# Two stages of an encoder layer: quadrant sums in scratch tiles, the first FFN set's weights split earlier

## The chip, the cores and the metric

The kernel runs on one core of one Trainium2 chip. The metric is the device time of one execution in microseconds (us). The kernel before takes 1883.55 us, the median of three runs (1881.67 to 1885.08).

## What is computed

The reference is a two-layer encoder over 512 tokens of width 1024, all in float32. Each layer mixes tokens with three kinds of attention, gates and merges them, and goes on so:

```python
mix = jnp.einsum('bsd,de->bse', merged, w_out[l])
x = layer_norm(DN_ALPHA * x + mix, ln1_g[l], ln1_b[l])
gu = jnp.einsum('bsd,df->bsf', x, w_ffn_in[l])
hidden = jax.nn.silu(gu[..., :D_FF]) * gu[..., D_FF:]
ffn = jnp.einsum('bsf,fd->bsd', hidden, w_ffn_out[l])
x = layer_norm(DN_ALPHA * x + ffn, ln2_g[l], ln2_b[l])
```

D_FF is 2816. The change lies between the first of these lines and the fourth.

## The kernel before, in words

**Number format.** Every matrix operand is split in two float32r parts, hi and lo, and a product is three matmuls: hi·hi, hi·lo and lo·hi (`mm3`, L158 to L161; `product`, L737 to L747). A split is a copy to hi on ScalarE and a subtraction to lo on VectorE. `split` (L189 to L195) does it in program order; `wsplit` (L137 to L143) does it for weights, into tiles `whi` and `wlo` of 1024 columns, four of each, and at high priority.

**Buffers.** Weights are loaded on SyncE's queue into tiles `raw` of 1024 columns, of which there are two (L127), or, in the fast FFN sets, into slots of H. H is a list of 8 slots of 1024 columns and R one of 38 slots of 512 columns (class `Slots`, L61 to L77): `get` takes the slot that was put back first, `put` appends. Scratch tiles P (`ptile`, L122) have 512 columns, four of them. PSUM banks have tags (`acc`, `sc`, `pv`, `tr`), two banks each. The framework adds the semaphores, and orders each engine's instructions by priority, which is program order unless raised, and by its own estimate of when they can start.

**Output projection** (`out_proj`, L670 to L681). It runs over two halves of 512 output columns; for each it loads four pieces of `w_out`, and for each of four token tiles runs 24 matmuls of 512 columns, 192 in all. The result is added to the residual `xt`, four slots of H that were reloaded before. `yield` hands a finished token tile of the second half to the norm.

**Norm** (`layer_norm`, L204 to L223, then `to_xt`, L228 to L234). For each token tile VectorE takes statistics, GpSimd computes the inverse root (L201, L202) and a shift (L214, L215), and the 1024 columns are scaled in two ways: the first 512 on VectorE (L222, L223), the others on ScalarE (L217) and GpSimd (L218, multiply by the gain; L219, add the bias). Gain and bias are two more slots of H (L240). TensorE then transposes the tile in two groups (L233), and ScalarE and VectorE split it (L191, L192) into `xth` and `xtl`, which hold the transposed activations.

**FFN.** The 22 blocks of 128 hidden columns are worked off in eleven sets of two, in chunks of 3, 3, 3 and 2 sets (L926). Set 0 is plain (`ffn_plain`, L758): four weight pieces through `raw` and `wsplit`, then 192 matmuls of 256 columns, for each half of the tokens first gate, then up, then `hidden` (L749). It needs the first two token tiles for its first half only. The other ten sets are fast (`ffn_fast`, L775): seven products of 24 matmuls of 256 columns in place of eight, in the manner of Strassen and Winograd. Three products read a quadrant of x itself (`from_x`), four read one of four sums of quadrants (`from_sum`: t1 to t4); the weights are combined as well: `s = u0 + u1`, `u0 = g0 - u0`, `g0 = s - g0` (L797 to L799, high priority), later `g1 = g1 - g0`. A set loads `g0`, `u0`, `u1` into H, takes `s` from H, and loads `g1` into `raw`.

**The sums** (`x_sums`, L699 to L729) are computed once per layer, after set 0: nine VectorE operations of 1024 columns on three slots of H, and eight splits of 512 columns, in the order t2, t1, t3, t4. The three slots go back to H at L728, after the last split, so the slots that `ffn_fast` takes next (L789, L790) are in part these.

Of the kernel before, what the change touches and what calls it, by code (L numbers as in the profile page):

```python
# [9 lines left out]
F32 = mybir.dt.float32  # L10
# [74 lines left out]
def trunk(ctx, tc, x, ln_in, w_in, feat, bias, lamv, w_mla, w_mlr, w_mlv, w_branch, w_out,  # L85
# [93 lines left out]
    class KTiles:  # L179
# [5 lines left out]
        def __getitem__(self, key):  # L185
            p, k, c = key
            return self.tiles[k][p, c]

# [481 lines left out]
    def out_proj(xt, mg, l):  # L670
        act = tuple(KTiles(m) for m in mg)
        for hf in range(2):
            c = slice(hf * 512, (hf + 1) * 512)
# [25 lines left out]
    def x_sums():  # L699

        four = lambda t: t.rearrange("p (k c) -> p k c", k=4)
        h = lambda kh, th: f32(quad(xth, kh, th))
        lo = lambda kh, th: f32(quad(xtl, kh, th))
        ts = [H.get() for _ in range(3)]
        t1, t2, d = (four(t) for t in ts)

        def halves(t):
            res = []
            for i in range(2):
                hl = (R.get(), R.get())  # L710
                split(*hl, t[:, i * 512:(i + 1) * 512])
                res.append(hl)
            return res

        V.tensor_sub(t1, h(0, 1), h(0, 0))
        V.tensor_sub(d, lo(0, 1), lo(0, 0))
        V.tensor_add(t1, t1, d)
        V.tensor_sub(t2, h(1, 1), t1)
        V.tensor_add(t2, t2, lo(1, 1))
        s2 = halves(ts[1])  # L720
        s1 = halves(ts[0])
        V.tensor_sub(d, t2, h(0, 0))
        V.tensor_sub(d, d, lo(0, 0))
        s3 = halves(ts[2])
        V.tensor_sub(t1, h(1, 0), t2)
        V.tensor_add(t1, t1, lo(1, 0))
        s4 = halves(ts[0])
        H.put(*ts)  # L728
        return s1, s2, s3, s4  # L729
# [28 lines left out]
    def ffn_plain(l, m):  # L758

        chs = []  # L760
        for base in (0, D_FF):
            c = slice(base + m * 128, base + (m + 2) * 128)
            chs.append(wload_ks(lambda a, e: [w_ffn_in[l, a:e, c]], 256, (4, 4)))
# [3 lines left out]
        for h in range(2):  # L767
# [4 lines left out]
            res.append(hidden(pg[h], pu[h]))  # L772
        return res

    def ffn_fast(l, m, sums):  # L775
# [19 lines left out]
        A.activation(p1, px, AF.Copy)  # L795
        with tc.high_priority():
# [11 lines left out]
        product(px, halved(g1), from_x(1, 0), False)  # L808
# [30 lines left out]
    for l in range(DEPTH):  # L839
# [81 lines left out]
        for t in out_proj(xt, mg, l):  # L921
# [4 lines left out]
        for c, (m0, n) in enumerate(CHUNKS):  # L926
            sets = []
            for i in range(n):
                m = 2 * (m0 + i)
                if m0 + i == 0:  # L930
                    sets.append(ffn_plain(l, m))
                    sums = x_sums()
                else:
                    sets.append(ffn_fast(l, m, sums))
# [107 lines left out]
```

## Time and profile before

| what | value |
|---|---|
| median of three runs | 1883.55 us |
| the profiled execution | 1883.03 us |
| its span, first to last instruction | 1881.3 us |
| mean granted TensorE clock | 0.989 of full |
| TensorE busy, matmul | 1817.8 us, 97% |
| VectorE busy | 1323.6 us, 70% |
| ScalarE busy | 911.9 us, 48% |
| GpSimd busy | 135.7 us, 7% |
| DMA, share of 16 engines | 34.2% |

In the profile PE is TensorE's matmul, PEld its weight load, DVE is VectorE, ACT ScalarE, POOL GpSimd and SP SyncE. A line such as L142 is a line of the kernel; the helpers' lines (L141, L142, L191, L192) serve many callers, so the tile names tell the stage. Matmul durations overlap, so starts tell the rate. "Idle before" with an arrow is the time that the engine stood still ahead of an instruction, and what ended it.

### The profile page before, as it was taken

To read this page: it belongs to the slowest core of one execution; us is meant where nothing else is said; L and a number is where in the kernel's file an instruction comes from. 1 tells how busy PE (TensorE), PEld (TensorE's weight loads), DVE (VectorE), ACT (ScalarE), POOL (GpSimd) and SP (SyncE) were. 2 spreads that over 40 slices of the span, in tenths; PEclk is the share of its full clock that TensorE was granted. 3 is DMA by queue.
4 is the path that set the end of the run, shared out by engine and by line. 5 is a ranking of instruction groups with operands and counts; after the bars stand their busy time and mean duration, and the time that the engine had idled before them with its cause. 6 is when DMAs were issued, how large, how long until landed. Compare 5 with 4: busy or idle time off the path is not lost.

```text
span 1881.3 us, 28600 instructions
## 1 busy us (share of the span) xinstructions
PE 1817.8 (97%) x11200; PEld 1621.9 (86%) x11200; DVE 1323.6 (70%) x2172; ACT 911.9 (48%) x1621; POOL 135.7 (7%) x217
## 2 busy tenths in 40 slices
PE   7999999999997899999999999999999979999997
PEld 5988899988887899999879888999888779999995
DVE  6488886666558877777646888766656578676766
ACT  3567776555424433333236677755554244333430
POOL 4100000000003000000031000000000210000001
PEclk9999999999999899999999999999999989999999
DMA  7453333233232232323355332322233223333331
GB/s 251 117 164 95 90 84 84 74 84 94 86 129 79 90 113 90 115 88 106 110 154 159 118 96 86 91 67 81 81 100 130 84 74 121 109 96 108 100 98 71
DMA packets 167767, 195.88 MB, mean 104 GB/s; under 512 B 8528, under 2 KB 132688, under 8 KB 167632
## 3 DMA queue, kind: packets, MB, share of 16 engines
q1 hardware_dynamic: 167632, 194.05, 34.2%
q8 instruction: 88, 1.44, 0.3%
q14 instruction: 47, 0.39, 0.1%
HBM read 177.24 MB, written 9.44 MB: 99 GB/s over the span
## 4 chain that ended last, share of the span: by engine, by line
PE 88%; DVE 5%; DMA 2%; issue 2%; ACT 1%; POOL 1%; SPq 0%; POOLq 0%; DVEq 0%; ACTq 0%
PE acc L159 18%; PE acc L160 18%; PE acc L161 18%; PE sc L746 11%; PE pv L746 8%; PE tr L617 2%; DVE wlo L142 1%; PE pv L460 1%; DMA f<-in_w_ffn_in_dram 1%; PE sc L446 1%; PE pv L625 1%; PE pv L624 1%; PE sc L601 1%; PE sc L600 1%; PE sc L602 1%
## 5 line engine op out<-in xcount | busy, mean ns | idle before, releaser
L141 ACT ACTIVATE whi<-raw 128x1024 fp32r<-128x1024 f32 (+4 forms) x254 | 262.5, 1034 | 292.9 <-PE acc L161 63.8
L142 DVE TENSOR_TENSOR wlo<-raw,whi 128x1024 fp32r<-128x1024 f32 (+4 forms) x254 | 304.8, 1201 | 136.3 <-ACT whi L141 133.2
L159 PE MATMUL acc<-xth,whi 128*128 128x512 f32 x512 | 204.0, 399 | 0.1
L141 ACT ACTIVATE whi<-f 128x1024 fp32r<-128x1024 f32 x100 | 104.5, 1056 | 204.8 <-PE acc L161 102.3
L160 PE MATMUL acc<-xtl,whi 128*128 128x512 f32 x512 | 202.6, 396 | 0.0
L161 PE MATMUL acc<-xth,wlo 128*128 128x512 f32 x512 | 202.6, 396 | 0.0
L746 PE MATMUL pv<-r,whi 128*128 128x256 f32 x960 | 177.3, 284 | 23.7 <-ACT whi L141 22.5
L160 PE MATMUL acc<-wlo,r 128*128 128x512 f32 (+1 forms) x504 | 196.4, 390 | 0.0
L161 PE MATMUL acc<-whi,r 128*128 128x512 f32 (+1 forms) x504 | 196.4, 390 | 0.0
L159 PE MATMUL acc<-whi,r 128*128 128x512 f32 (+1 forms) x504 | 193.8, 390 | 2.3 <-DVE f L831 1.5
L159 PE MATMUL acc<-whi,xth 128*128 128x256 f32 (+2 forms) x576 | 174.9, 305 | 2.4 <-ACT whi L141 1.6
L160 PE MATMUL acc<-wlo,xth 128*128 128x256 f32 (+2 forms) x576 | 175.7, 306 | 1.0 <-DVE wlo L142 0.8
L161 PE MATMUL acc<-whi,xtl 128*128 128x256 f32 (+2 forms) x576 | 176.0, 306 | 0.0
L746 PEld LDWEIGHTS pv<-r,whi 128*128 128x128 f32 x960 | 150.0, 191 | 26.4 <-ACT whi L141 22.9
L142 DVE TENSOR_TENSOR wlo<-f,whi 128x1024 fp32r<-128x1024 f32 x100 | 121.2, 1222 | 31.0 <-ACT whi L141 31.0
L746 PE MATMUL pv<-r,wlo 128*128 128x256 f32 x480 | 135.7, 283 | 0.0
L746 PE MATMUL sc<-xth,whi 128*128 128x256 f32 x480 | 133.9, 280 | 0.0
L746 PE MATMUL sc<-xtl,whi 128*128 128x256 f32 x480 | 133.8, 279 | 0.0
L746 PE MATMUL sc<-xth,wlo 128*128 128x256 f32 x480 | 133.1, 279 | 0.0
L201 POOL TENSOR_SCALAR ring<-ring 128x1 f32<-128x1 f32 x68 | 26.3, 387 | 1417.2 <-ACT otmp L466 811.7
L159 PEld LDWEIGHTS acc<-whi,xth 128*128 128x128 f32 x576 | 109.1, 190 | 7.2 <-ACT whi L141 2.0
L160 PEld LDWEIGHTS acc<-wlo,xth 128*128 128x128 f32 x576 | 109.2, 190 | 6.4 <-DVE wlo L142 2.1
(225 smaller groups left out, 4308.5 us busy)
## 6 DMA issues: line engine op xcount, KB each, us to landing
raw<-in_w_in_dram SPq DMA_DIRECT2D x64, 512.0 KB, 3.8
f<-in_w_ffn_in_dram SPq DMA_DIRECT2D x60, 512.0 KB, 3.6
raw<-in_w_ffn_out_dram SPq DMA_DIRECT2D x44, 512.0 KB, 3.8
raw<-in_w_in_dram SPq DMA_DIRECT2D x64, 256.0 KB, 3.3
raw<-in_w_ffn_in_dram SPq DMA_DIRECT2D x28, 512.0 KB, 3.6
raw<-in_w_branch_dram SPq DMA_DIRECT2D x24, 512.0 KB, 3.5
raw<-in_w_out_dram SPq DMA_DIRECT2D x16, 512.0 KB, 3.9
r<-r SPq DMA_DIRECT2D x56, 128.0 KB, 2.9
```

The lines of the kernel that those rows point to most:

```text
L141: A.activation(hi[:, :n], raw[:, :n], AF.Copy)
L142: V.tensor_sub(lo[:, :n], raw[:, :n], f32(hi[:, :n]))
L159: T.matmul(o, lh[0], rh[0], start=first, stop=False)
L160: T.matmul(o, lh[0], rh[1], start=False, stop=False)
L161: T.matmul(o, lh[1], rh[0], start=False, stop=last)
L201: G.tensor_scalar(dst, src, eps, None, op0=OP.add)
L446: T.matmul(sc, qs[j][:, tsl(t)], ks[j][1], start=False, stop=True)
L460: T.matmul(po[:, 0:256], ch_[:, tsl(k)], v, start=k == 0, stop=False)
L600: T.matmul(sc, q[0][:, tsl(t)], k[0], start=True, stop=False)
L601: T.matmul(sc, q[0][:, tsl(t)], k[1], start=False, stop=False)
L617: T.transpose(pt[:, tsl(i)], prs[i % 2][:, tsl(kp + i // 2)], ident)
L746: T.matmul(o[:, c], w[a][:, j, f], x[e], start=fresh and mi == 0 and j == 0 and n == 0, stop=j == 3 and n == 2, skip_group_check=True)
```

## The change

The sums are computed in two rounds (i = 0, 1), each over two of the four blocks of 128 in a quadrant, in three scratch tiles P of 512 columns instead of three slots of H. The weights of set 0 are loaded and split by a new function at the start of the second half of `out_proj`, into 16 slots of R, two operations of 512 columns per piece, in place of `whi` and `wlo`; the slots go back to R when set 0 is done. In the first fast set only, the first product with `g1` moves from fifth to second place. The diff, without the unchanged lines between:

```diff
+    class Pairs:
+        def __init__(self, tiles, ncol):
+            self.tiles, self.ncol = tiles, ncol
+        def __getitem__(self, key):
+            p, k, c = key
+            a = k % 2 * self.ncol
+            return self.tiles[k // 2][p, a + c.start:a + c.stop]
+    def wload_slots(src_of, ncol, steps):
+        res, slots, k = [], [], 0
+        for n in steps:
+            raw = wp.tile([128, 1024], F32, tag="raw", name="raw", bufs=2)
+            rv = raw[:, :n * ncol].rearrange("p (k c) -> p k c", k=n)
+            c = 0
+            for src in src_of(k * 128, (k + n) * 128):
+                w = src.shape[1]
+                nc.sync.dma_start(rv[:, :, c:c + w], src.rearrange("(k p) c -> p k c", p=128))
+                c += w
+            hl = ([], [])
+            for a in range(0, n * ncol, 512):
+                hi, lo = R.get(), R.get()
+                split(hi, lo, raw[:, a:a + 512])
+                hl[0].append(hi)
+                hl[1].append(lo)
+            slots += hl[0] + hl[1]
+            res.append((k, n, tuple(Pairs(i, ncol) for i in hl)))
+            k += n
+        return res, slots
...
     def gate_tiles():
         return [dp.tile([128, 512], F32, tag="gt", name="gt", bufs=2) for _ in range(2)]
 
-    def out_proj(xt, mg, l):
+    def out_proj(xt, mg, l, ahead):
         act = tuple(KTiles(m) for m in mg)
         for hf in range(2):
+            if hf == 1:
+                ahead()
             c = slice(hf * 512, (hf + 1) * 512)
             ch = wload_ks(lambda a, e: [w_out[l, a:e, c]], 512, (2, 2, 2, 2))
             for t in range(NT):
...
 
     def x_sums():
 
-        four = lambda t: t.rearrange("p (k c) -> p k c", k=4)
         h = lambda kh, th: f32(quad(xth, kh, th))
         lo = lambda kh, th: f32(quad(xtl, kh, th))
-        ts = [H.get() for _ in range(3)]
-        t1, t2, d = (four(t) for t in ts)
-        def halves(t):
-            res = []
-            for i in range(2):
+        two = lambda t: t.rearrange("p (k c) -> p k c", k=2)
+        res = [[], [], [], []]
+        for i in range(2):
+            ts = [ptile() for _ in range(3)]
+            t1, t2, d = (two(t) for t in ts)
+            q = lambda a: a[:, 2 * i:2 * i + 2]
+            def halves(n, t):
                 hl = (R.get(), R.get())
-                split(*hl, t[:, i * 512:(i + 1) * 512])
-                res.append(hl)
-            return res
-        V.tensor_sub(t1, h(0, 1), h(0, 0))
-        V.tensor_sub(d, lo(0, 1), lo(0, 0))
-        V.tensor_add(t1, t1, d)
-        V.tensor_sub(t2, h(1, 1), t1)
-        V.tensor_add(t2, t2, lo(1, 1))
-        s2 = halves(ts[1])
-        s1 = halves(ts[0])
-        V.tensor_sub(d, t2, h(0, 0))
-        V.tensor_sub(d, d, lo(0, 0))
-        s3 = halves(ts[2])
-        V.tensor_sub(t1, h(1, 0), t2)
-        V.tensor_add(t1, t1, lo(1, 0))
-        s4 = halves(ts[0])
-        H.put(*ts)
-        return s1, s2, s3, s4
+                split(*hl, t)
+                res[n].append(hl)
+            V.tensor_sub(t1, q(h(0, 1)), q(h(0, 0)))
+            V.tensor_sub(d, q(lo(0, 1)), q(lo(0, 0)))
+            V.tensor_add(t1, t1, d)
+            V.tensor_sub(t2, q(h(1, 1)), t1)
+            V.tensor_add(t2, t2, q(lo(1, 1)))
+            halves(1, ts[1])
+            halves(0, ts[0])
+            V.tensor_sub(d, t2, q(h(0, 0)))
+            V.tensor_sub(d, d, q(lo(0, 0)))
+            halves(2, ts[2])
+            V.tensor_sub(t1, q(h(1, 0)), t2)
+            V.tensor_add(t1, t1, q(lo(1, 0)))
+            halves(3, ts[0])
+        return res
 
     def from_x(kh, th):
         return lambda j: (quad(xth, kh, th)[:, j], quad(xtl, kh, th)[:, j])
...
         split(*hl, sg)
         return hl
 
-    def ffn_plain(l, m):
-        chs = []
+    def plain_weights(l, m):
+        chs, slots = [], []
         for base in (0, D_FF):
             c = slice(base + m * 128, base + (m + 2) * 128)
-            chs.append(wload_ks(lambda a, e: [w_ffn_in[l, a:e, c]], 256, (4, 4)))
+            ch, sl = wload_slots(lambda a, e: [w_ffn_in[l, a:e, c]], 256, (4, 4))
+            chs.append(ch)
+            slots += sl
+        return chs, slots
+    def ffn_plain(chs, slots):
         pg = [bank("sc"), bank("sc")]
         pu = [bank("pv"), bank("pv")]
         res = []
...
                     gemm_w(pp[h][:, mi * 256:(mi + 1) * 256], w, slice(mi * 128, (mi + 1) * 128), XT,
                            slice(h * 256, (h + 1) * 256), KD)
             res.append(hidden(pg[h], pu[h]))
+        R.put(*slots)
         return res
 
-    def ffn_fast(l, m, sums):
+    def ffn_fast(l, m, sums, early):
 
 
         t1, t2, t3, t4 = sums
...
         product(px, halved(g0), from_x(0, 0), True)
         p1 = ptile()
         A.activation(p1, px, AF.Copy)
+        if early:
+            product(px, halved(g1), from_x(1, 0), False)
         with tc.high_priority():
             V.tensor_add(s, u0, u1)
             V.tensor_sub(u0, g0, u0)
...
         u3 = ptile()
         V.tensor_add(u3, py, p1)
         V.tensor_add(u3, pz, u3)
-        product(px, halved(g1), from_x(1, 0), False)
+        if not early:
+            product(px, halved(g1), from_x(1, 0), False)
         with tc.high_priority():
             V.tensor_sub(g1, g1, g0)
         product(pz, halved(g1), from_x(1, 1), False)
...
             xt.append(H.get())
             nc.sync.dma_start(xt[t], xd[t])
         gb = load_gb(ln1[l])
-        for t in out_proj(xt, mg, l):
+        plain = []
+        for t in out_proj(xt, mg, l, lambda: plain.append(plain_weights(l, 0))):
             layer_norm(xt[t], *gb, spread=SP1[t])
             to_xt(xt[t], t)
         H.put(*gb)
...
             for i in range(n):
                 m = 2 * (m0 + i)
                 if m0 + i == 0:
-                    sets.append(ffn_plain(l, m))
+                    sets.append(ffn_plain(*plain[0]))
                     sums = x_sums()
                 else:
-                    sets.append(ffn_fast(l, m, sums))
+                    sets.append(ffn_fast(l, m, sums, m0 + i == 1))
                 if done is not None and i < 2:
                     for _ in ffn_down(l, *done, xt, c == 1, i):
                         pass
```

## Rows read from the trace of the kernel before

**Rows 1.** The page: chain that ended last by engine; a tensor's DMA issues

```profile
PE 88%; DVE 5%; DMA 2%; issue 2%; ACT 1%; POOL 1%; SPq 0%; POOLq 0%; DVEq 0%; ACTq 0%
...
raw<-in_w_out_dram SPq DMA_DIRECT2D x16, 512.0 KB, 3.9
```

**Rows 2.** Waits of the whole run: engine, line, releaser, us in total, times, longest us

```profile
PE pv L746 <- ACT whi L141: 22.5, 2, 11.3
```

**Rows 3.** Timeline of TensorE: start us, us, what, idle before and its releaser

```profile
576.29 0.39 PE L159 MATMUL sc<-xth,whi 128*128 128x256 f32 x1 [3.25 <-ACT xth L191]
...
616.21 0.58 PE L746 MATMUL pv<-r,whi 128*128 128x256 f32 x1 [11.33 <-ACT whi L141]
...
947.54 0.69 PE L233 MATMUL tr<-cons,f 128*128 128x128 f32 x2 [3.21 <-DVE xtl L192]
```

**Rows 4.** Stretches: us; busy us of PE, PEld, DVE, ACT, POOL; granted clock; DMA share; GB/s

```profile
526.80:572.60 45.80, 45.80 (x203) 36.80 (x202) 25.31 (x34) 10.52 (x12) 10.30 (x14) 1.00 0.24 79
575.00:580.00 5.00, 3.51 (x26) 3.08 (x27) 4.75 (x6) 4.29 (x6) 2.57 (x2) 1.00 0.35 105
588.00:608.00 20.00, 16.89 (x144) 16.68 (x142) 19.46 (x24) 8.30 (x14) 0.00 (x0) 1.00 0.15 50
608.00:616.00 8.00, 0.00 (x0) 0.00 (x0) 3.84 (x4) 0.90 (x1) 0.00 (x0) 0.56 0.21 66
616.00:623.00 7.00, 6.63 (x30) 6.34 (x31) 6.17 (x6) 3.48 (x5) 0.00 (x0) 0.53 0.44 131
623.00:660.00 37.00, 37.00 (x317) 37.00 (x316) 31.42 (x35) 17.68 (x21) 0.00 (x0) 1.00 0.29 90
```

**Rows 5.** Chain that ended last, in order of time: start us, us, what

```profile
598.81 1.14 DVE f L722
...
605.15 2.42 DVE r L192 x4
...
607.59 3.48 DMA f<-in_w_ffn_in_dram
...
611.20 1.24 DVE f L797
...
617.96 4.69 PE pv L746 x22
...
626.36 2.83 PE pv L746 x24
```

**Rows 6.** Timeline of SyncE's queue: start us, us, what

```profile
523.63 0.38 SPq L132 DMA_DIRECT2D raw<-in_w_out_dram  x1
...
553.96 21.25 SPq L132 DMA_DIRECT2D raw<-in_w_ffn_in_dram  x4
...
586.44 36.04 SPq L782 DMA_DIRECT2D f<-in_w_ffn_in_dram  x6
```

**Rows 7.** Timeline of GpSimd in the norm: start us, us, what, idle before

```profile
561.90 0.57 POOL L202 TENSOR_TENSOR ring<-ring,expo 128x1 f32<-128x1 f32 x1
...
570.34 1.55 POOL L202 TENSOR_TENSOR ring<-ring,expo 128x1 f32<-128x1 f32 x1
...
583.65 1.39 POOL L218 TENSOR_TENSOR f<-f,f 128x512 f32<-128x512 f32 x1 [0.94 <-ACT f L217]
```

**Rows 8.** Timeline of VectorE in the norm and at the sums' start

```profile
569.99 1.47 DVE L142 TENSOR_TENSOR wlo<-raw,whi 128x1024 fp32r<-128x1024 f32 x1 [1.10 <-ACT whi L141]
...
587.68 0.69 DVE L192 TENSOR_TENSOR xtl<-tr,xth 128x512 fp32r<-128x512 f32 x1 [3.79 <-ACT xth L191]
588.29 1.22 DVE L715 TENSOR_TENSOR f<-xth 128x1024 f32<-128x1024 f32 x1
```

**Rows 9.** Groups by form, 584 to 625: shapes, count, busy us, mean ns, idle before

```profile
L192 DVE TENSOR_TENSOR r<-f,r 128x512 fp32r<-128x512 f32 x8 | 5.1, 685 | 0.0
...
L191 ACT ACTIVATE r<-f 128x512 fp32r<-128x512 f32 x8 | 4.7, 622 | 4.9 <-DVE f L723 4.4 <-DVE f L717 0.5
```

**Rows 10.** Timeline of ScalarE in the projection: start us, us, what, idle before

```profile
545.20 1.06 ACT L141 ACTIVATE whi<-raw 128x1024 fp32r<-128x1024 f32 x1 [14.84 <-PE acc L161]
```

## The prediction, made before the change was run

> **What bounds the kernel now.** The page comes first: TensorE carries 88% of the chain that ended last [rows 1]. A change off TensorE's path gives nothing, so I looked for the places where TensorE stands still. The waits name the longest: `product` (L746) waits for a weight split on ScalarE twice, 22.5 us together, 11.3 us the longest, once in each layer [rows 2]; in order of time it ends at 616.21 in layer 0 [rows 3]. [...] A smaller stop lies ahead of it: the first FFN matmul, at 576.29, waits 3.25 us for ScalarE to split a transposed block [rows 3].
>
> The chain in order of time says why the long stop exists [rows 5]. The last four splits of `x_sums` end at 607.6; only then can the load of `u0` be issued, since `x_sums` held three slots of H and `u0` and `u1` take two of them. The load costs 3.48 us, three VectorE additions of 1.24 us follow from 611.20, then a ScalarE copy, and TensorE starts again. VectorE was not the cause in the end: of 608 to 616 it works 3.84 us [rows 4]. SyncE shows the same from the other side: six loads spread over the 36 us after 586.44, held for slots [rows 6].
>
> **The change, part by part** (layer 0; the waits say that layer 1 stops as long).
>
> 1. Sums in scratch tiles instead of H. Following the slot queue by hand, four of H's eight slots hold the residual and two the norm's gain and bias at this place; two are free, last used by the merges. Now `g0` and `u0` get those two, `u1` the gain's and `s` the bias's. The gain is last read by GpSimd's multiply for the last token tile, which ends at 585.0 [rows 7]; `u1` can be issued then and, with the 3.5 us of the load just read, lands by 589, some 22 us before 611. The wait for the DMA disappears. Late next is `t2`, the sum that the second kind of product reads, so VectorE has to be counted. In the chain an operation of 1024 elements takes 1.13 us from start to start, one of 512 takes 0.605 us [rows 5]. Eighteen half sums cost 10.9 us where nine whole ones cost 10.2; the eight splits stay. The sums start at 588.29, after 3.79 us in which VectorE waits for the last token block [rows 8]. Up to `t2` VectorE has 13 operations of the first half (nine sums, four splits), 6 of the second and 4 of the plain set's two `hidden` calls, 23 × 0.605 = 13.9 us; the three additions and the split of the new `g0`, 4 × 1.13 = 4.5 us; 18.4 in all, to 606.7. Splitting `g0` and `g1` adds 2.3 us if it isn't done before: 609.0.
>
>  [...] The sum above goes by the starts.
>
> 2. `early`: one more product, 24 matmuls, stands ahead of `t2`. It is only moved: 24 matmuls cost 2.83 us [rows 5]. TensorE came to its stop 11.33 us before 616.21 [rows 3], at 604.9; now it reaches `t2` at 607.7. The moved product writes the bank that `p1` is copied from, so it waits for that copy, 0.62 us on ScalarE [rows 9], and for one of four scratch tiles. I cost that at 0.5 us.
>
> 3. The plain set's weights in R during the output projection. Four splits of 1024 leave the norm's stretch (1.06 us on ScalarE [rows 10], 1.2 to 1.5 us on VectorE [rows 8]); eight of 512, 0.62 and 0.685 us each [rows 9], come into the projection. There TensorE runs 45.8 us without a stop [rows 4], and ScalarE is idle for 14.84 us up to 545.20 [rows 10]; the added 5 us of each engine lie beside that. Of the 16 slots of R, fourteen were last read long before, and two by the merge that ends as the projection begins, 526.8. The loads change places: SyncE issued the first piece of the second half's `w_out` at 523.63 and the plain set's four from 553.96 [rows 6]; now the plain set's go first through the same two `raw` tiles. A piece takes 3.9 us to land [rows 1] and about 2.6 us to split, 6.5 us for two in flight, so four need some 13 us, from 523.6 to between 537 and 540, and `w_out`'s first two pieces land at 541 to 544. They were split at 545.20, when their target tiles came free [rows 10]. Nothing lost, but the slack is about 1 us; what a late queue would cost stands among the rivals.
>
> 4. The norm's stretch without those splits. Its stop of 3.25 us hangs on a chain through GpSimd, whose one-column power took 0.57 us alone [rows 7] and 1.55 us while VectorE split a weight [rows 7, 8]. Bounds: nothing gained, since at the end of layer 0 a norm of the same form stops TensorE for 3.21 us [rows 3], and all of 3.25. The splits of `g0` and `g1` may move into this place, since their target tiles are free once the projection ends. I take 1.0, the power's own delay, which is nearer the unchanged row.
>
> 5. The lower clock after the long stop. 22 matmuls took 4.69 us where 24 at full clock take 2.83 [rows 5]: 2.1 us lost; half of the 6.2 us from 616.21 to the clock's rise would be 3.1. I take 2.6. It goes only if the stop shrinks: the stretch around the 3.25 us stop kept clock 1.00, after 11.3 us it was at half [rows 4].
>
> After `t2` VectorE has little air: from 623 to 660 it was busy 31.4 of 37 us, 85%, with the sums already done [rows 4]. Now some 3.6 us of sums go into the same time. I book 1.5 us of new short stops per layer, the copy's 0.5 among them; bounds 0 and, in the first rival, 6.5.
>
> **Sum** per layer: 11.3 (stop) + 2.6 (clock) + 1.0 (norm) − 1.5 (new stops) = 13.4 us; two layers 26.8. The profiled execution took 1883.03 us with a span of 1881.3; it becomes 1856.2. The median of the runs, 1883.55, is 0.5 above that execution, so the forecast is **1856.7 us**, 1.4% faster. All bounds at their best (11.3 + 3.1 + 3.25, twice) give 1848.2.
>
> **Rivals.**
>
> *VectorE takes over the same stop.* Four scratch tiles serve two rounds of three, two `hidden` tiles and `p1`, so the second round may wait for the first, and every split then shows its ScalarE copy (0.62 us) instead of hiding it: 6 × 0.62 = 3.7 us on top of 609.0, so `t2` at about 613 and a stop of 4 to 6.5 us, after which the clock may be low again. Gain per layer: 11.3 − 6.5 + 1.0 = 5.8 us at worst, 11.3 − 4 + 1.0 = 8.3 at best; 1867 to 1872 us. For it: VectorE works 19.46 of 20 us from 588 to 608 [rows 4]. Against: part of its work can move into the 3.79 us of idle time that ends at 587.68 [rows 8].
>
> *`w_out` comes late: slower.* Place: SyncE's queue and the two `raw` tiles. If the plain set's splits are ordered behind work that ends late, `raw` isn't freed and the second half's weights wait with it. The point that decides: TensorE needs the first of them halfway through the projection's 45.8 us, at 549.7 [rows 4]; landing (3.9) and splitting (2.3) put the last moment of issue at 543.5. If the splits only run once the norm has begun, at 561.9 [rows 7], the stop is 561.9 + 6.2 − 549.7 = 18.4 us plus 2.6 of clock per layer, less the 13.4 gained: 7.6 us per layer lost, 1898.8 us. Against it: ScalarE's idle time, slots that are free by 526.8, and program order, in which these splits stand ahead of the norm.
>
> *No change that can be told.* Within 0.2% (3.8 us, what a measurement of this kernel can tell from none) it stays if the next waiter refills the long stop to within 1.9 us a layer. With `u0` and `u1` over 20 us earlier I see no row for that.
>
> **How the numbers follow.** Forecast (1848 to 1864) 0.70; VectorE's stop (1864 to 1879) 0.19; no change 0.05; late `w_out` 0.06. Faster by over 0.2%: 0.70 + 0.19 = 0.89. The range starts at the sum of the best bounds, 1848, and ends at 1871, inside the first rival: 0.70 and some two thirds of 0.19, about 0.82.
>
> **What would show it.** Right: no wait of `product` on a ScalarE split over 4 us near 605; clock 1.00 from 600 to 640; `u1`'s load issued near 585; VectorE over 90% busy from 588 to 640; the plain set's splits between 527 and 545, none after 560; the projection still 45.8 us. Wrong: a stop in the projection's second half (late `w_out`), or one of 4 us or more ahead of the first matmul that reads a sum, with VectorE busy through it (first rival). If the long stop is gone and the time still fell by under 15 us, the next two sets are where to look for what came back.

## The result, and the profile after

The changed kernel takes **1870.45 us** (median of 5 runs, 1868.85 to 1874.65) against 1883.55 us: ratio 0.994, 95% interval 0.9923 to 0.9958. Its profiled execution, the fastest of the five, took 1868.85 us with a span of 1867.1 us, 14.2 us less than the span before. The forecast was 1856.7 us; the time lies at the upper end of the range, and the gain, 13.1 us, is a little under half of the 26.8 forecast. What happened is nearly the first rival: VectorE took over a part of the stop. Line numbers of the changed kernel: sums L750 to L761, products L780, `wsplit` L141 and L142, other splits L224 and L225, the three additions L839 to L841, `g1 - g0` L853, evacuation of the projection L713, loads of the plain set L209 and of a fast set L822.

The page, chain that ended last by engine (answers to [rows 1]; TensorE 88% before):

```profile
PE 87%; DVE 4%; DMA 3%; POOL 2%; ACT 2%; issue 1%; SPq 0%; POOLq 0%; DVEq 0%; ACTq 0%
```

Timeline of TensorE (answers to [rows 3]):

```profile
538.91 0.50 PE L159 MATMUL acc<-whi,r 128*128 128x512 f32 x1 [1.11 <-DVE f L713]
...
577.36 0.39 PE L159 MATMUL sc<-xth,r 128*128 128x256 f32 x1 [3.27 <-ACT xth L224]
...
610.38 0.58 PE L780 MATMUL sc<-r,whi 128*128 128x256 f32 x1 [3.46 <-ACT r L224]
```

Three stops: a new one in the projection, the norm's, which is what it was (3.25), and the long one, now 3.46 us where it was 11.33 and ended by the split of a sum, not by a weight. Layer 1 has the same three (1.12, 3.26 and 3.47 us).

Stretches (columns as in [rows 4]):

```profile
526.80:572.60 45.80, 44.69 (x197) 35.63 (x196) 28.45 (x40) 14.47 (x20) 9.25 (x13) 1.00 0.43 143
...
588.00:608.00 20.00, 18.91 (x160) 18.71 (x158) 19.61 (x26) 7.44 (x11) 0.00 (x0) 1.00 0.19 53
608.00:616.00 8.00, 5.62 (x25) 5.43 (x26) 7.83 (x13) 2.98 (x5) 0.00 (x0) 0.61 0.21 66
616.00:623.00 7.00, 7.00 (x59) 7.00 (x59) 4.70 (x6) 3.66 (x4) 0.00 (x0) 0.96 0.26 78
```

In 608 to 616 VectorE now works 7.83 of 8 us (3.84 before): what ends the stop is no longer a load but VectorE's work. The clock still falls, to 0.61 there. The chain in order of time shows what VectorE did last and what the low clock costs:

```profile
605.54 1.07 ACT whi L141
606.63 1.22 DVE wlo L142
607.85 0.60 DVE P L751
608.46 0.60 DVE r L225
609.06 0.61 DVE P L752
609.69 0.64 ACT r L224
610.38 6.19 PE sc L780 x26
```

26 matmuls take 6.19 us; at the 2.83 us for 24 of [rows 5] they would take 3.07, so 3.1 us are lost, as much as before. In layer 1 the same stop ends at 1534.96 and the clock is back sooner, which halves that loss to an estimated 1.6 us, half of the time between (stretch):

```profile
1538.20:1540.20 2.00, 2.00 (x19) 2.00 (x19) 1.90 (x4) 1.39 (x3) 0.00 (x0) 1.00 0.03 8
```

L752 in the chain is the last addition of `t1`. So what TensorE waits for is the second half of `t1`; that of `t2` is added two microseconds later, at 610.97. And the early product, which the forecast had ahead of this stop, stands behind it. Timelines of VectorE, ScalarE and TensorE:

```profile
608.98 0.68 DVE L752 TENSOR_TENSOR P<-P 128x512 f32<-128x512 f32 x1
...
610.97 0.69 DVE L754 TENSOR_TENSOR P<-P,xtl 128x512 f32<-128x512 f32 x1
...
609.69 0.63 ACT L224 ACTIVATE r<-P 128x512 fp32r<-128x512 f32 x1 [2.58 <-DVE P L752]
610.23 0.58 ACT L835 ACTIVATE P<-sc 128x512 f32<-128x512 f32 x1
...
610.86 0.58 PE L780 MATMUL sc<-xth,whi 128*128 128x256 f32 x1
```

L835 is the copy of `px` into the scratch tile `p1`; the early product writes that bank and starts as the copy ends. On ScalarE the copy comes directly behind the split of `t1`, for which ScalarE had stood idle 2.58 us. Whether its own scratch tile was free sooner, the trace doesn't tell. What ran ahead of the stop were 12 matmuls on the first halves of `t1` and `t2`, from 605.39. VectorE's timeline has the rest:

```profile
536.96 1.29 DVE L225 TENSOR_TENSOR r<-raw,r 128x512 fp32r<-128x512 f32 x2 [2.62 <-ACT r L224]
538.17 1.28 DVE L713 SCALAR_TENSOR_TENSOR f<-f,acc 128x512 f32<-128x512 f32 x2
...
571.05 1.48 DVE L142 TENSOR_TENSOR wlo<-f,whi 128x1024 fp32r<-128x1024 f32 x1 [1.10 <-ACT whi L141]
...
588.03 1.23 DVE L839 TENSOR_TENSOR f<-f,f 128x1024 f32<-128x1024 f32 x1 [2.15 <-DMA f<-in_w_ffn_in_dram]
...
592.28 1.23 DVE L853 TENSOR_TENSOR raw<-raw,f 128x1024 f32<-128x1024 f32 x1
...
594.02 2.35 DVE L142 TENSOR_TENSOR wlo<-f,whi 128x1024 fp32r<-128x1024 f32 x2
...
596.89 0.69 DVE L750 TENSOR_TENSOR P<-xth 128x512 f32<-128x512 f32 x1
```

The first sum starts at 596.89, not at 588.29 as before [rows 8]: the additions, `g1 - g0` and two weight splits now stand ahead of it. At 571.05 the split of the new set's `g0` stands where a plain split stood. At 538.17 the evacuation that TensorE waits for stands behind a split whose load was late.

### The profile page after: what moved, and what is told of

The parts are those of the page before. It is cut to its first block, busy times and chain, and to the rows that moved or that the text cites. A ratio compares the mean times of both kernels' runs of the same rounds, so it can differ in the third digit from the quotient of the medians.

```text
span 1867.1 us, 28608 instructions
## 1 busy us (share of the span) xinstructions
PE 1818.0 (97%) x11200; PEld 1622.1 (87%) x11200; DVE 1324.6 (71%) x2198; ACT 915.3 (49%) x1629; POOL 134.9 (7%) x217
## 4 chain that ended last, share of the span: by engine, by line
PE 87%; DVE 4%; DMA 3%; POOL 2%; ACT 2%; issue 1%; SPq 0%; POOLq 0%; DVEq 0%; ACTq 0%
PE acc L159 17%; PE acc L160 17%; PE acc L161 17%; PE sc L780 11%; PE pv L780 8%; DVE wlo L142 2%; PE tr L650 2%; PE pv L493 1%; DMA raw<-in_w_ffn_in_dram 1%; DMA f<-in_w_ffn_in_dram 1%; PE sc L479 1%; PE pv L658 1%; PE pv L657 1%; ACT whi L141 1%; PE sc L634 1%
## 5 line engine op out<-in xcount | busy, mean ns | idle before, releaser
L141 ACT ACTIVATE whi<-raw 128x1024 fp32r<-128x1024 f32 (+4 forms) x246 | 254.2, 1034 | 261.6 <-PE acc L160 49.4
L142 DVE TENSOR_TENSOR wlo<-raw,whi 128x1024 fp32r<-128x1024 f32 (+4 forms) x246 | 292.9, 1192 | 126.2 <-ACT whi L141 122.9
L141 ACT ACTIVATE whi<-f 128x1024 fp32r<-128x1024 f32 x100 | 104.7, 1056 | 188.8 <-PE acc L161 84.1
L780 PE MATMUL pv<-r,whi 128*128 128x256 f32 x960 | 173.9, 280 | 1.4 <-DVE P L848 1.4
L780 PEld LDWEIGHTS pv<-r,whi 128*128 128x128 f32 x960 | 148.0, 188 | 3.2 <-issue 2.1
L142 DVE TENSOR_TENSOR wlo<-f,whi 128x1024 fp32r<-128x1024 f32 x100 | 121.8, 1227 | 30.7 <-ACT whi L141 30.6
L780 PE MATMUL sc<-xth,whi 128*128 128x256 f32 x480 | 135.9, 283 | 0.0
L780 PE MATMUL sc<-xtl,whi 128*128 128x256 f32 x480 | 135.3, 282 | 0.0
L780 PE MATMUL sc<-xth,wlo 128*128 128x256 f32 x480 | 134.9, 282 | 0.0
L780 PE MATMUL pv<-r,wlo 128*128 128x256 f32 x480 | 134.0, 279 | 0.0
L159 PEld LDWEIGHTS acc<-whi,r 128*128 128x128 f32 x504 | 94.2, 188 | 26.1 <-DVE f L713 3.1
```

The costliest lines, as they stand in the source:

```text
L141: A.activation(hi[:, :n], raw[:, :n], AF.Copy)
L142: V.tensor_sub(lo[:, :n], raw[:, :n], f32(hi[:, :n]))
L159: T.matmul(o, lh[0], rh[0], start=first, stop=False)
L780: T.matmul(o[:, c], w[a][:, j, f], x[e], start=fresh and mi == 0 and j == 0 and n == 0, stop=j == 3 and n == 2, skip_group_check=True)
```

## The experiments

All were timed against the kernel before on the same chip. Their line numbers lie up to 37 above those of the changed kernel; operations and tiles keep their names. In the diffs `behind(i)` issues what it holds after instruction i on the same engine; it orders a queue and adds no wait.

### Parts undone

**The sums back in H** (the rest of the change stays).

```diff
-        for i in range(2):
-            ts = [ptile() for _ in range(3)]
+        ts = [H.get() for _ in range(3)]
...
+        H.put(*ts)
```

> The sums go back into three slots of H, undivided; the early split of the weights and the early product stay. Theory A (the scratch tiles removed the wait for the slots, and what is left of the long stop is VectorE's queue) expects the long stop back: 11.33 us less the 2.8 us of the early product, so about 8.5 us in each layer, ended by the load of u0 or u1, and the low clock after it as in the kernel before. Against the changed kernel's 1870.45 us that is 2 x (8.5 - 3.46) = 10 us more, less 2 x 1.11 us if the short stop in the projection goes with the early loads of g0 and u0: 1878 to 1881 us. Theory B (the scratch tiles gave nothing; the gain of 13 us came from the weights and the early product) expects the changed kernel's time, 1869 to 1872 us, and a stop near 3.5 us.

Measured: 1871.88 us, ratio 0.9923 (0.9911 to 0.9934), not slower than the changed kernel, where Theory A had 1878 to 1881. Its long stop is 0.69 and 5.77 us, longer as Theory A has it, though short of its 8.5, but the norm's stop is gone but for three pieces of 1.1 us together:

```profile
575.83 0.63 PE L266 MATMUL tr<-cons,f 128*128 128x128 f32 x4 [0.43 <-DVE xtl L225]
576.85 0.39 PE L159 MATMUL sc<-xth,r 128*128 128x256 f32 x1 [0.39 <-ACT xth L224]
...
577.65 0.66 PE L266 MATMUL tr<-cons,f 128*128 128x128 f32 x4 [0.30 <-DVE xtl L225]
```

With three slots of H held by the sums, `g0` is not loaded early, so its split and that of `g1` come at 589 us, after the norm. The time alone would have said "the scratch tiles are worth nothing"; the trace shows two effects that oppose each other.

**The weights back after the norm.**

```diff
-        for t in out_proj(xt, mg, l, lambda: plain.append(plain_weights(l, 0))):
+        for t in out_proj(xt, mg, l, lambda: None):
...
-                    sets.append(ffn_plain(*plain[0]))
+                    sets.append(ffn_plain(*old_weights(l, m)))
```

> The first set's weights are loaded and split at their old place, after the norm; sums in scratch and the early product stay. Theory A (the early weights freed room in the norm's stretch that the splits of g0 and g1 took at once, so the norm's stop did not shrink) expects the norm's stop unchanged at 3.2 to 3.3 us, the 1.11 us stop in the projection gone (the kernel before has none), and the splits of g0 and g1, 2.3 us of VectorE, now behind the plain set's: the long stop grows from 3.46 to between 4.5 and 6 us. In all 1870.45 - 2.2 + 2 x (1.0 to 2.5) = 1870 to 1873 us. Theory B (the early weights carry the gain) expects the kernel before's long stop, and 1880 us or more.

Measured: 1880.67 us, 0.9973 (0.9963 to 0.9984). The projection has no stop and the norm's is 3.27 us, as Theory A had it, but ahead of the sums' products TensorE now stops four times, 3.24, 1.56, 1.16 and 2.24 us, 8.2 in all instead of 3.46; I had allowed 6. So the early weights carry some 6 us of the gain (0.994 to 0.9973). The longer stops suggest that they do it by relieving VectorE behind the norm, where I had counted nothing for them.

**The early product back.**

```diff
-                    sets.append(ffn_fast(l, m, sums, m0 + i == 1))
+                    sets.append(ffn_fast(l, m, sums, False))
```

> The second product of the first fast set goes back to its old place behind the three products that read sums; the rest of the change stays. Theory (t2 is late by VectorE's own count, whatever TensorE does) expects TensorE at its stop 2.83 us earlier and the stop longer by as much, 3.46 + 2.8 = 6.3 us in each layer, with the product's time given back behind it, so that only the clock's loss counts: 2.83 us x 2 later at most, ratio to the kernel before 0.993 to 0.997. Rival (the early product holds t2 back, since it takes a bank and its copy a scratch tile) expects the stop unchanged or shorter and a ratio of 0.990 to 0.993.

Measured: 1874.81 us, 0.9948 (0.9935 to 0.996). Stop 4.59 us, not 6.3: in the changed kernel the early product stands behind the stop, so taking it away can't lengthen the stop by its own length. The norm's stop had also shrunk to 1.41 us by another order, so the time can't be read alone. It was run again below.

### Two queue orders

**The splits of `g0` and `g1` behind the norm's last scaling.**

```diff
-        product(px, halved(g0), from_x(0, 0), True)
+        with behind(scaled):
+            w0 = halved(g0)
+        product(px, w0, from_x(0, 0), True)
```

> One order alone: the splits of g0 and g1 are issued behind the last scaling of the norm, where e2_sums_in_h had them by chance and its stops at the norm summed to 1.1 us in place of 3.27. Theory (those two splits on VectorE, and the slow GpSimd operations beside them, are the norm's stop of 3.27 us) expects 1.1 us here too, and the long stop longer by no more than 1.1 us, since VectorE idles 2.15 us for u1 in that place: 2 to 4 us in all less than the changed kernel, ratio 0.991 to 0.992. Rival (the stop at the norm is its own chain through GpSimd, and e2_sums_in_h lost it for another reason) expects 3.2 to 3.3 us as before, and a ratio of 0.993 to 0.995.

Measured: 1867.61 us, 0.9908 (0.9895 to 0.9922). Timelines of TensorE and of GpSimd:

```profile
577.03 0.63 PE L270 MATMUL tr<-cons,f 128*128 128x128 f32 x4 [0.45 <-DVE xtl L228]
578.05 0.38 PE L159 MATMUL sc<-xth,r 128*128 128x256 f32 x1 [0.39 <-ACT xth L227]
...
578.86 0.66 PE L270 MATMUL tr<-cons,f 128*128 128x128 f32 x4 [0.31 <-DVE xtl L228]
```

```profile
573.91 0.57 POOL L238 TENSOR_TENSOR ring<-ring,expo 128x1 f32<-128x1 f32 x1
```

The stop falls from 3.27 to 1.15 us, and the power takes 0.57 us. In the changed kernel it had taken 1.55 beside the split at 571.05:

```profile
571.40 1.55 POOL L235 TENSOR_TENSOR ring<-ring,expo 128x1 f32<-128x1 f32 x1
```

It starts at 571.40 and ends at 572.95, 0.42 us after the split's end at 572.53. Why the power takes longer beside a split was not shown.

The time understates what this order gives: the stop in the projection was longer here, 2.14 and 1.63 us in the two layers against 1.11 and 1.12, and the clock was at 0.50 behind the longer one (541 to 543 us).

**The third and fourth plain splits behind the evacuation.**

```diff
-                split(hi, lo, raw[:, a:a + 512])
+                with behind(after):
+                    split(hi, lo, raw[:, a:a + 512])
```

> One order alone: the splits of the first set's second weight piece are issued behind the evacuation of the projection's second token tile. Theory (the 1.1 us stop in the projection is that evacuation standing in VectorE's queue behind a split that waits for its load) expects this stop gone in both layers, and 2 us less than the changed kernel: ratio 0.992. Rival (the evacuation is late because of its bank or the shared DMA queues) expects the stop to stay at 1 us or more, and the ratio at 0.993.

Measured: 1864.41 us, 0.99 (0.9885 to 0.9915). The stop is gone; stretch and VectorE's timeline:

```profile
526.80:572.60 45.80, 45.80 (x203) 36.89 (x202) 30.01 (x42) 15.05 (x20) 10.33 (x14) 1.00 0.44 148
```

```profile
536.96 0.69 DVE L718 SCALAR_TENSOR_TENSOR f<-f,acc 128x512 f32<-128x512 f32 x1 [2.00 <-PE acc L161]
```

The evacuation now waits for TensorE and no longer TensorE for it. The span is 5.8 us shorter, where the two stops make 2.2. Some 1.6 us more can be put down, as an estimate, to half of a stretch at the low clock, 903.3 to 906.5 us, that the changed kernel's profile has and this one has not (granted clock 0.50 against 1.00). The rest is not located; the changed kernel's own five runs lie up to 5.8 us apart.

**Both orders.**

> The orders of nrm_splits_behind and evac_first together; nothing else differs from the changed kernel. Theory (the stop at the norm and the stop in the projection are two queue orders on VectorE, and do not feed each other) expects both gone, the 3.46 us stop and the low clock behind it left as they were, and the two gains added: ratio 0.988 (0.9908 + 0.990 - 0.993). Rival (time won ahead of the FFN is lost again at the next stop, since the sums wait for VectorE anyway) expects the long stop to grow and a ratio of 0.990 or more.

Measured: 1862.03 us, 0.9875 (0.9862 to 0.9888). The gains add, and the long stop stays at 3.46 us. On this base the parts could be weighed again:

> both_orders with the sums back in three slots of H, undivided. e2_sums_in_h had hidden what the scratch tiles are worth, because it lost the norm's stop by chance. Theory (scratch tiles shorten the long stop, 6.4 us there against 3.46) expects the long stop 5.8 to 6.5 us, and 2 x 3 = 6 us more than both_orders: ratio 0.991. Rival (the scratch tiles are worth nothing, since VectorE sets the time either way) expects the time of both_orders within 2 us.

Measured: 1868.18 us, 0.991 (0.9897 to 0.9923), 6.2 us more than both orders on the same chip; the stop is 0.69 and 5.62 us:

```profile
612.57 0.80 PE L787 MATMUL pv<-r,whi 128*128 128x256 f32 x2 [5.62 <-ACT whi L141]
```

> both_orders with the second product of the first fast set back behind the three that read sums. Theory (early work for TensorE shortens the long stop by its own 2.8 us, as far as VectorE does not lose by it) expects the long stop at 4.6 us, as e1 had it, or up to 6.3, and 2 to 6 us more than both_orders: ratio 0.989 to 0.991. Rival (the early product only moves the wait) expects the time of both_orders within 2 us.

Measured: 1866.32 us, 0.99 (0.9887 to 0.9914), against 0.9875 some 4.7 us more. The stop is 1.13 us longer and a new one of 1.05 us comes later; 2 x 2.18 = 4.4 us. The Theory's reason did not hold: TensorE comes to the stop 0.16 us earlier (605.01 us, 605.17 in both orders), not 2.8. What changed is VectorE's queue. From the first addition of the weights to the last addition of `t1` it holds eight operations of 1024 columns instead of seven, a split of `g1` being the added one, and that last addition starts at 608.20 instead of 607.24. Timelines of TensorE and of VectorE:

```profile
609.60 0.39 PE L786 MATMUL sc<-r,whi 128*128 128x256 f32 x1 [4.59 <-ACT r L228]
...
642.82 0.39 PE L786 MATMUL sc<-xth,whi 128*128 128x256 f32 x1 [1.05 <-ACT P L792]
```

```profile
604.72 1.23 DVE L142 TENSOR_TENSOR wlo<-raw,whi 128x1024 fp32r<-128x1024 f32 x1 [0.15 <-ACT whi L141]
...
608.20 0.69 DVE L758 TENSOR_TENSOR P<-P 128x512 f32<-128x512 f32 x1
```

### The stop ahead of the sums' products

The expectations call it the stop before t2; what TensorE awaits there in the changed kernel is the second half of `t1`, as shown above.

**More scratch.**

```diff
-            ts = [ptile() for _ in range(3)]
+            ts = [ptile(), keep[i], ptile()]
```

> The sum t2 of each half gets a tile of its own (the gate tiles, idle here), so the sums take four tiles in turn from the ring of four instead of six; no instruction is added or moved by hand. Theory A (VectorE's queue: the three additions, the new g0 and the splits stand ahead of the second half's sums) expects no change: stop 3.2 to 3.7 us, 1868 to 1872 us. Rival (the four scratch tiles hold the second half back until the first is split) expects the stop under 1 us, the clock kept at 1.00, and 2 x (3.46 + 3.1) = 13 us less: 1857 us.

Measured: 1874.72 us, 0.9943 (0.9928 to 0.9958): no gain. But the framework changed TensorE's order with it, and the stop gave way to stops of 2.89 us (the early product, on the copy of `px`) and 1.01 us. The copy itself waited for one of VectorE's splits (timeline of ScalarE):

```profile
613.48 0.60 ACT L836 ACTIVATE P<-sc 128x512 f32<-128x512 f32 x1 [1.51 <-DVE r L225]
```

By the program the copy has only one thing to wait for in such a split, the scratch tile that the split reads, so the scratch tiles still hold work back here. As a control of the order the run is inconclusive, and it does not clear the tiles. Its projection also had a stop of 2.52 us in layer 0.

**VectorE's order, three attempts.** `s7_order` issues the additions behind the second half's `t2`, and `g1 - g0` behind all sums; it also puts `t2` into the gate tiles, moves the plain set's second `hidden` back, and takes the bank `pz` later. An excerpt:

```diff
-        with tc.high_priority():
+        with tc.high_priority(), behind(early):
             V.tensor_add(s, u0, u1)
```

> VectorE's order alone: the sums that the second and fourth products read (t1, t2 of both halves) come first, the three additions and the new g0 behind them, then the plain set's second hidden multiply, the other two sums after that, and g1 - g0 last. t2 lies in the gate tiles, as in ring_more_scratch, which is this run's control. Theory A (the rest of the long stop is the order of VectorE's queue) expects t2 ready at 601 to 604 us, ahead of TensorE, which comes at about 606: a stop under 1 us, the clock kept at 1.00 through 608 to 618, and 2 x (3.46 + 3.1 - 0 to 1) = 11 to 13 us less than 1870.45: 1857 to 1860 us. Rival (VectorE has too much work in any order, so the stop only moves to the product behind the new g0) expects a stop of 3 us or more ahead of the fourth product, the clock low again, and 1866 to 1872 us.

Measured: 1872.25 us, 0.9927 (0.9914 to 0.994). No stop ahead of the sums' products, and full clock up to 622; then 2.92 us before the product of `g1 - g0`. Part of the time was lost elsewhere: in layer 0 the projection stopped for 2.50 us, with the clock at 0.50 in 542 to 545. The next attempt moved `g1 - g0` up and the third sum ahead of `u0`'s split:

```diff
-        end = rest() if early else None
+        end = third() if early else None
...
+        with behind(end):
+            w = halved(u0)
...
-        with tc.high_priority(), behind(end):
+        with tc.high_priority():
             V.tensor_sub(g1, g1, g0)
```

> s7_order with its last stop taken up: there VectorE stood idle 3.3 us behind a split of u0 that waited for a slot of the split weights, and g1 - g0 stood behind all sums, which stopped TensorE 2.9 us in place of the 3.46 before t2. Here g1 - g0 follows the additions at once, and the third sum comes before the split of u0. Theory (VectorE has enough time for all of it, and the stops are only its order) expects no stop over 1 us from 590 to 640 and the clock at 1.00 all through: 2 x (3.46 + 3.1) = 13 us less than the changed kernel, less up to 2 us: ratio 0.986 to 0.988. Rival (each cure of one stop makes the next, since VectorE is full from 588 to 625) expects again some 3 us at one of the following products and a ratio of 0.992 to 0.994.

Measured: 1875.25 us, 0.995 (0.9937 to 0.9962): one stop of 4.93 us, where the next set's first product waits for a `silu` that waits for a scratch tile. Then that product was issued behind this set's last one:

```diff
-        product(px, halved(g0), from_x(0, 0), True)
+        w = halved(g0)
+        with behind(ahead and ahead[0]):
+            product(px, w, from_x(0, 0), True)
```

> s9_order2 with the order of TensorE tied too: there the next set's first product stood ahead of g1's and u1's last ones and waited 4.93 us for its bank; here it is issued behind them, and the next set's additions behind the fourth sum. Theory (the long stop is order and not lack of time) expects no stop over 1.5 us from 590 to 640 and the clock at 1.00: 2 x (3.46 + 3.1) = 13 us less than the changed kernel, less 2 x 1: ratio 0.987 to 0.988. Rival (VectorE is full, and the stop moves on again) expects a stop of 3 us or more between 616 and 645, a low clock behind it, and 0.992 to 0.995.

Measured: 1876.68 us, 0.9955 (0.9941 to 0.9969). Here too the projection lost more than in the changed kernel: 2.24 and 2.25 us in the two layers, each with the clock at 0.50 behind it (540.2 to 543.4, 1468.5 to 1471.8).

> s11_tensor_order and both_orders in one. If each theory holds, the gains add: 0.988 of both_orders less the 0.0055 of the long stop, ratio 0.982 to 0.984, some 1851 us where the kernel before takes 1883.55. If the rival of s11_tensor_order holds, the ratio stays at 0.987 to 0.989.

Measured: 1865.91 us, 0.9896 (0.9883 to 0.9908); both have one stop of 6.64 us. In the order s7, s9, s12, timelines of TensorE:

```profile
622.89 0.50 PE L793 MATMUL pv<-r,whi 128*128 128x256 f32 x2 [2.92 <-ACT whi L141]
```

```profile
622.07 0.58 PE L795 MATMUL sc<-xth,whi 128*128 128x256 f32 x1 [4.93 <-ACT P L801]
```

```profile
619.68 0.58 PE L799 MATMUL sc<-xth,whi 128*128 128x256 f32 x1 [6.64 <-DVE P L885]
```

Each time the stop moved to the next dependence, as the rivals had it (a late weight, a held scratch tile, a bank not yet emptied).

**Less work instead of another order.** Third and fourth sum left out:

```diff
-            V.tensor_sub(d, t2, q(h(0, 0)))
...
-        return res
+        return res[0], res[1], res[1], res[0]
```

> both_orders with the third and fourth sums left out (t2 and t1 are read in their place), so VectorE has eight half sums and four splits fewer, 7.2 us, and ScalarE four copies fewer; the output is not the layer's. Six of those twelve instructions stood ahead of the second half's t2, 3.6 us. Theory (VectorE's work ahead of t2 is the long stop) expects it gone or under 0.5 us, the clock at 1.00 behind it, and 2 x (3.46 + 3.1) = 13 us less than both_orders: ratio 0.9805 to 0.982. Rival (the stop is the chain of u1's load, additions, split and product, whatever the sums cost) expects it over 2 us and a ratio over 0.985.

Measured: 1853.54 us, 0.9833 (0.9819 to 0.9846). With nothing tied beyond both orders, the stop ahead of the sums' products is gone and the clock stays at 1.00 from 584 to 660:

```profile
612.91 0.51 PE L780 MATMUL pv<-r,whi 128*128 128x256 f32 x2 [0.86 <-DVE P L848]
```

So with less of VectorE's work ahead of them the sums are ready before TensorE needs them, as the Theory has it; the rival, the chain of `u1`, is out. Two things changed along with that work and are not told apart from it: the sums left out hold no scratch tiles, and the copy of `px` comes at 604.84, so that the early product runs from 607.13. The gain is 8 us instead of 13; 2 x (0.86 + 0.58) of it went into two new stops (the second at 656), and in layer 1 both_orders had lost only about half of the 3.1 us to the clock (0.50 in 1529 to 1532).

**The filler.** To `s12_all_orders`: the additions that empty the bank come first, the fourth sum is made in place, and TensorE's order is free again.

```diff
-                t1, t2 = two(a), two(keep[i])
-                V.tensor_sub(t1, q(h(1, 0), i), t2)
+                t2 = two(keep[i])
+                V.tensor_sub(t2, q(h(1, 0), i), t2)
...
+        with tc.high_priority():
             V.tensor_add(u3, py, p1)
```

> s12_all_orders with its stop of 6.63 us taken up: there the product of g1 - g0 waited for two VectorE additions that empty its bank, which stood behind the next set's three, and the next set's first product could not fill in, since a scratch tile for the silu that frees its bank was held by the fourth sum. Here the two additions come first, the fourth sum is made in the gate tile in place, and TensorE's order is left to the scheduler, which puts the next set's first product into that hole. Theory (order and scratch alone make the stops after t2) expects no stop over 1 us from 590 to 640 and the clock at 1.00: both_orders less 10 to 13 us, ratio 0.981 to 0.982. Rival (VectorE is full through this stretch, and the stop moves on once more) expects a stop of 2.5 us or more and a ratio over 0.985.

Measured: **1852.67 us**, 0.9827 (0.9814 to 0.9841), the fastest version, 33 us under the kernel before with all its work. Stretches, and the one stop left there:

```profile
588.00:608.00 20.00, 20.00 (x173) 20.00 (x172) 19.75 (x27) 8.61 (x12) 0.00 (x0) 1.00 0.24 77
608.00:616.00 8.00, 6.63 (x57) 6.46 (x57) 7.09 (x10) 4.17 (x6) 0.00 (x0) 1.00 0.23 75
616.00:623.00 7.00, 7.00 (x62) 7.00 (x61) 6.08 (x7) 2.01 (x2) 0.00 (x0) 1.00 0.00 0
```

```profile
612.54 0.47 PE L797 MATMUL pv<-r,whi 128*128 128x256 f32 x2 [1.37 <-DVE P L874]
```

VectorE does the same work as in the changed kernel, 19.75 of 20 us, and TensorE does not stop for it until 611: VectorE is full, but not too slow. Here the copy of `px` starts at 603.96 and the early product at 605.57, ahead of the product of `t1`, much as the forecast had it. My expectation of no stop over 1 us was missed by 0.37, the ratio by 0.0007.

## Why the prediction was wrong

Per layer, the sum against what the trace shows:

| Term | forecast | found |
|---|---|---|
| Long stop removed | 11.3 | 11.3 |
| Clock after it | 2.6 | 0 |
| Norm | 1.0 | 0 |
| New stops | -1.5 | -4.57 (3.46 + 1.11) |
| Sum | 13.4 | 6.7 |

This is layer 0; the stops of layer 1 give 11.21 - 3.47 - 1.12 = 6.6. Together 13.3, between the 13.1 of the medians and the 14.2 of the spans.

- **Right:** that the wait for `u0` and `u1` is one for slots of H and goes (`u1` was issued at 584.43, I said 585.0), and that VectorE is late next. Late `w_out`, the rival with the slowdown, did not come.
- **Right by luck:** TensorE arrived at the stop at 606.92, forecast 607.7. The forecast had the 24 matmuls of the early product run first; what ran were 12 matmuls on the first halves of the sums.
- **The step that failed: "I book 1.5 us of new short stops".** They came to 4.57 us, 3.46 of it ahead of the sums' products. The 1.5 stood on the count of VectorE up to `t2`, 18.4 us from 588.29 to 606.7. VectorE works from 588.03 with one pause of 0.19 us, adds `t1`'s second half until 609.66 (21.6 us) and `t2`'s until 611.66 (23.6 us). What I had left out stood in the queue ahead at high priority: `g1 - g0`, the splits of `s` and of `u0`, 3 x 1.13 us; and a last transposed block, 0.6 us: 18.4 + 4.0 = 22.4. The rest is mostly steps that depend on the one before and start 0.67 to 0.72 us apart. I had counted what `t2` needs, not what is ahead of it. Three runs show the queue from different sides: in e1_in_both one more operation of 1.23 us ahead of `t1` makes the stop 1.13 us longer; in n0_two_sums six instructions fewer ahead, and in s13_filler the same work in another order with more scratch, take it away.
- **A second step, in part 2:** "now it reaches `t2` at 607.7", with the early product done and 0.5 us for its copy. The copy started at 610.23 and the early product at 610.86, behind the stop, so TensorE stood idle with 24 matmuls still to do. How much of the 3.46 us the product would have filled in its place was not tested by itself.
- **The clock, 2.6 us.** "It goes only if the stop shrinks": it shrank to 3.46 us and the clock fell all the same. The row I leaned on, 3.25 us at clock 1.00, was no bound: in the same trace the stop of 3.21 us at 947.54 [rows 3], which the prediction itself names, was followed by the clock at 0.50 (row below). This term and the new stops are one mistake with two prices, 3.1 + 2.6 us of the missing 6.7.
- **The norm, 1.0 us.** I had written that the splits of `g0` and `g1` may move into this place, and taken the gain nevertheless. They did, to the same engine, within 1.1 us of the old start [rows 8]. nrm_splits_behind shows what was there to be had: 2.1 us a layer.
- **The plain set's weights, booked as hidden.** I looked for a slip of `w_out`; what slipped was an evacuation on VectorE, 1.11 us, behind a split that waited for its load (evac_first). That the early weights relieve VectorE after the norm, some 6 us in all, I had not counted either.
- **The chances.** The first rival, 0.19, had the mechanism and the time: 1867 to 1872 us. It gave the four scratch tiles as a reason; the runs show the order of VectorE's queue, and leave the tiles' share open.
- **The price of a VectorE operation.** I priced 512 columns by the starts, 0.605 us [rows 5]. Inside the sums, independent operations start 0.60 us apart (604.55 to 605.15) and dependent ones 0.72 (597.50 to 598.22); the whole duration of a split of 512 columns is 0.685 [rows 9]. It is a matter of 0.1 us per operation and did not decide.

## What to carry to other kernels

When a stop is ended by a load, count for the engine that comes next everything that its queue holds ahead of the awaited result, raised instructions first, and not only what the result needs. Work moved out of a crowded place leaves a hole, and the next work whose data are early can go into it, as the split of `g0` did at 571.05: say what that is before you book the gain. A product that the program moves ahead runs ahead only if all that it waits for, here a copy on another engine that started at 610.23, comes in time. An undone part whose time doesn't change may be two effects that cancel; only the trace of that run tells.

## What was not expected of the hardware

The same stop at the norm left the clock at 1.00 in layer 0 of the changed kernel (3.27 us, at 577.36) and halved it in layer 1 of the same execution (3.26 us). The stretch behind the first, then the second stop and the stretch behind it:

```profile
578.00:580.00 2.00, 2.00 (x19) 1.98 (x18) 1.62 (x5) 1.09 (x2) 1.61 (x3) 1.00 0.00 0
```

```profile
1500.38 0.44 PE L159 MATMUL sc<-xth,r 128*128 128x256 f32 x1 [3.26 <-ACT xth L224]
```

```profile
1502.00:1504.00 2.00, 2.00 (x11) 2.00 (x10) 1.41 (x3) 1.12 (x2) 1.09 (x2) 0.50 0.00 0
```

In evac_first it was halved in layer 0, and in the kernel before behind the stop of 3.21 us at 947.54 (stretches of the two, in this order):

```profile
578.00:580.00 2.00, 2.00 (x12) 2.00 (x11) 1.96 (x4) 0.35 (x1) 1.60 (x3) 0.50 0.00 0
```

```profile
948.00:950.00 2.00, 2.00 (x8) 1.71 (x7) 1.93 (x5) 0.60 (x1) 2.00 (x3) 0.50 0.81 244
```

Stops of 2.14 us (nrm_splits_behind: clock 0.50 in 541 to 543), 2.89 us (ring_more_scratch: clock 0.50 in 616 to 618) and 3.46 us (changed kernel: clock 0.50 in 610.38 to 612) were followed by the low clock too; one of 2.52 us (ring_more_scratch, projection: clock 1.00 in 541.8 to 544.8) and one of 1.37 us (s13_filler: clock 1.00 in 608 to 616) were not. So the stops of 2 to 3.5 us here cost their own length, or up to nearly twice that (3.46 + 3.1 us), and which was not to be told from the length. What decides it stays open here.
